# Both feed-forwards with early halves: even features first on one token half, five products more for their pairs, and 24 modulation columns moved into the mixing

## The chip, the cores and the metric

The kernel runs on one core of a Trainium2 chip. The metric is device time in microseconds for one execution. A core has TensorE (matmuls, PE in the profile), VectorE (DVE), ScalarE (ACT), GpSimd (POOL) and SyncE (SP, which here issues the DMAs). Each engine runs its own list of instructions in order and waits on semaphores that others raise. Matmul results go to PSUM, a small memory in banks of 128 x 512 fp32 numbers, which ScalarE and VectorE can read and write too.

## The reference

One layer over 1024 latent tokens and 256 context tokens, width 1024: a half-step feed-forward, a token mixing of two recurrent kinds, a second half-step feed-forward. Every step is modulated by columns computed from the condition vector `c`.

```python
def swiglu(h, w1, w3, w2):
    return (jax.nn.silu(h @ w1) * (h @ w3)) @ w2
...
    m_l = jnp.split(cond_lat @ ada_w[i] + ada_b[i], N_MOD, axis=-1)
    x = x + 0.5 * m_l[2][:, None, :] * swiglu(modulate(rms_norm(x, norm1_w[i]), m_l[0], m_l[1]),
                                                ffn1_w1[i], ffn1_w3[i], ffn1_w2[i])
    ctx = ctx + 0.5 * m_c[2][:, None, :] * swiglu(modulate(rms_norm(ctx, norm1_w[i]), m_c[0], m_c[1]), ...)
    y_l, y_c = token_mixing(modulate(rms_norm(x, norm2_w[i]), m_l[3], m_l[4]), ...)
    x = x + m_l[5][:, None, :] * y_l
    x = x + 0.5 * m_l[8][:, None, :] * swiglu(modulate(rms_norm(x, norm3_w[i]), m_l[6], m_l[7]),
                                                ffn2_w1[i], ffn2_w3[i], ffn2_w2[i])
return rms_norm(x, final_norm_w)
```

The hidden width is 2816, that is 22 features of 128 columns, 11 pairs of features. The modulation `cond_lat @ ada_w` has 72 columns of 128 for the latents, numbered 8m+k for part m and k = 0..7.

## The kernel before, in words

**Numbers.** Every fp32 product is made of three fast matmuls. An operand is split into a high part, written by ScalarE (`whi`, L421), and a low part, the difference, written by VectorE (`wlo`, L422). `mm3` (L426 to L428) then issues high x high, low x high and high x low into one bank. A weight half, `raw`, is a 128 x 512 tile loaded from HBM, split into `whi` and `wlo`; there are six slots of each.

**Seven products.** The activations of 1024 tokens are cut into two token halves and two halves of the inner width. A pair of features makes a 2 x 2 block of weights, and `chain` (L706 ff.) computes the 2 x 2 block product with seven block products in place of eight. A block product, here simply a product, is 4 `mm3`, so 12 matmuls of 128 x 512. The weight combinations are made by VectorE in `seven_w` (L687 to L694), the activation combinations `t1` to `t4` once per feed-forward. Partial results are copied from PSUM by ScalarE (`keep`, L711) and added by VectorE (`plus`, L715). A pair has one chain for w1, whose results go through silu (`c_silu`, L738), and one for w3, whose results are multiplied with it (`c_mul`, L743). When the four gated blocks of a pair are there, `g_out` forms their combinations by subtractions (L751) and stores them to `gd` in HBM (L752), for the products with w2 later. `w2_sums` loads three w2 blocks (L792), adds them and stores the sums.

**The first features.** Before the activations of the second token half are ready, features are computed the classic way, one at a time, half by half: four in the first feed-forward (`first1`, then a loop that finishes token half 1) and two in the second (`first2`). The other 9 and 10 pairs go through `hidden`, which runs w1 chain, modulation work, `w2_sums`, w3 chain, and modulation work again for each pair.

**Modulation.** The 72 latent columns are dot products of a 128 x 1024 block of `adaT` with the condition row: one DMA and one VectorE multiply-and-reduce (L523) each, hung into the chains, `MPER` of them after each chain.

**Order.** In `first1` the three computing engines follow the program's order. In the chains a scheduler orders each engine's list by priority; loads of weights have a raised one (`WPRI`). In the mixing a planner (`Recorder`) records operations and emits a list by its own costs; `SEQ` is the list of steps that it runs through.

Of the kernel before, what the change touches and what calls it, by code (L numbers as in the profile page):

```python
# [392 lines left out]
class Trunk:  # L393
    def __init__(self, ctx, tc, I, out, outt):
        self.tc, self.nc, self.I, self.out, self.outt = tc, tc.nc, I, out, outt
        self.ctx = ctx
        self.uid = 0
        self.ns, self.ndg = NS, 2
        self.cp = ctx.enter_context(tc.tile_pool(name="cp", bufs=1))
        self.hp = ctx.enter_context(tc.tile_pool(name="hp", bufs=1))  # L400
        self.mixd = self.nc.dram_tensor("mixd", (D, LAT), F32, kind="Internal").ap()
        self.xd = self.nc.dram_tensor("xd", (D, LAT), F32, kind="Internal").ap()
        self.gds = [self.nc.dram_tensor(f"gd{i}", (8, NP, P, 512), F32, kind="Internal").ap() for i in range(2)]
        self.sds = [self.nc.dram_tensor(f"sd{i}", (2, NP, P, 512), F32, kind="Internal").ap() for i in range(2)]
        for n, s in (("cgk", (256, CTX)), ("crk", (512, CTX)), ("cgv", (CTX, 512)), ("crv", (CTX, 512)), ("p89d", (P, CTX)), ("s0g", (4, P, P)),
                     ("s0r", (4, P, 2, P)), ("rvd", (P, 8, 256))):
            setattr(self, n, self.nc.dram_tensor(n, s, F32, kind="Internal").ap())
# [135 lines left out]

    def mod_fin(self, j, s, one=False):
# [88 lines left out]
    def norm_t(self, tg, a, b, pool, tp):  # L633
# [8 lines left out]
        for k in range(4):  # L642
            t = self.norm_k(tg, k, a, b, rb, pool)
# [91 lines left out]

    def c_silu(self, f, tg, t, new=False):
# [12 lines left out]
    def g_out(self, f):  # L749
# [11 lines left out]
        put(1, b11), put(2, b21), put(3, b22)  # L761
# [54 lines left out]
    def hidden(self, f0, mods=lambda: None, hold=False):  # L816
        for f in range(f0, NF, 2):
            if hold and f == NF - 2:
                self.held = []
            self.chain(self.w1, f, self.c_silu, self.psA)  # L820
            if f > f0:
                mods()
            self.w2_sums(f // 2 - 1)
            self.chain(self.w3, f, self.c_mul, self.psB)
            if f > f0:
                mods()
# [139 lines left out]
    def ffn_open(self, i, gates, pool):  # L966
        self.w1, self.w3, self.w2 = (self.I[f"w{i}{j}"] for j in (1, 3, 2))
        self.gates_m, self.fp, self.s, self.g = gates, pool, {}, {}
# [176 lines left out]
    def first2(self, tp, diag):  # L1145
        t3 = [self.tile(tp, [P, 512], F32R, f"t3l{k}") for k in range(4)]
        t3 = [tuple(t3[2 * i:2 * i + 2]) for i in range(2)]
        ws = {}
        for f in range(2):
            for i, w in ((0, self.w1), (1, self.w3)):  # L1150
                ws[f, i] = self.load_halves(w[f], t3 if (f, i) == (1, 1) else (None, None))
        raw = []
        for tg in LATTG:
            for f in range(2):
                ps = self.psA()
                mms = self.proj(ws[f, 0], tg, ps)
                if tg == f == 0:
                    self.tc.add_manual_dep(diag.ins, mms[HELD].ins.name, SCHED, reason="order")
                self.c_silu(f, tg, ps, True)
                if tg:  # L1160
                    raw.append(self.t34_raw(2 * f))
                self.c_mul(f, tg, self.H(ws[f, 1], tg))
                if tg:
                    raw.append(self.t34_raw(2 * f + 1))
        return raw

    def first1(self, pools, n1):
# [10 lines left out]
        def fetch(i, q):  # L1178
            raws[i, q] = self.raw_half((self.w1, self.w3)[i % 2][i // 2][:, 512 * q:512 * q + 512])
# [20 lines left out]
        def mms(i, k, js):  # L1200
            w, h = self.wslice(ws[i], k), self.h[0][k]
            for j in js:
                u, v = ((0, 0), (0, 1), (1, 0))[j]
                nc.tensor.matmul(pss[i], w[u], h[v], start=k == 0 and j == 0, stop=k == KD - 1 and j == 1)
# [89 lines left out]
        for st in range(1, KD):  # L1294
# [10 lines left out]
            for i in range(6):  # L1305
                mms(i, st, (0, 2, 1))
                if i == 2 * (st == 1) and n < KD:
# [11 lines left out]
                if n == KD:  # L1319
# [3 lines left out]
                    if i == 2:  # L1323
                        self.c_mul(0, 0, pss[1])
                        self.c_silu(1, 0, pss[2], True)
# [7 lines left out]
        self.c_mul(1, 0, pss[3])  # L1333
        self.c_silu(2, 0, pss[4], True)
        ps = self.psA()
        for k in range(KD):
            if k == 2:
                pr = self.rstd_rows(r, 512, n1, dg=dg)
            self.mm3(ps, self.wslice(ws[6], k), self.h[0][k], k == 0, k == KD - 1)
        rb[1] = self.scr(n1, "nrb")  # L1340
        nc.scalar.copy(rb[1], pr)
        norm_a = lambda k: self.norm_a(1, k, a, b, rb[1], n1, self.x[1][k])
        norm_a(0)
        for k in range(KD):
            if k + 1 < KD:
                norm_a(k + 1)
            if k == 2:
                self.c_mul(2, 0, pss[5])
                self.c_silu(3, 0, ps, True)
            self.norm_b(1, k, b, self.x[1][k])  # L1350
        self.c_mul(3, 0, self.H(ws[7], 0))
        return ws
# [553 lines left out]
    def lat_phase(self, pool):  # L1906
# [32 lines left out]
        cr = lambda: [self.ctx_ret(h, pool) for h in range(4)]  # L1939
        for s in SEQ:  # L1940
            eval(s, {**globals(), **locals()})
        self.late_sg = {h: self.gate_proj(I["wrg"][h], pool) for h in (2, 3)}
# [88 lines left out]
    def run(self):  # L2031
# [26 lines left out]
        self.alloc_h((0, 1), self.hp)  # L2058
        with tc.manual_schedule(engines={mybir.EngineType.PE, mybir.EngineType.DVE, mybir.EngineType.Activation}):
            ws = self.first1((xp, xp, None), n1)  # L2060
            cls("n1"), cls("f1w")
            self.tp = tp = opn("tp")
            t_steps = self.t_make(xp, tp)
            for f in range(4):
                self.c_silu(f, 1, self.H(ws[2 * f], 1), True)
                next(t_steps)
                self.c_mul(f, 1, self.H(ws[2 * f + 1], 1))
                if f % 2:
                    next(t_steps)
# [12 lines left out]
        self.hidden(4, lambda: mods(MPER), True)  # L2082
# [119 lines left out]
        self.x[0] = [rec.wrap(t, xp) for t in self.x[0]]  # L2202
        self.h[2] = [tuple(rec.wrap(t, hc) for t in p) for p in self.h[2]]
# [34 lines left out]
        rec.run()  # L2238
        self.ndg = 2
# [16 lines left out]
        self.T = [[], [], [], []]  # L2256
        for i, raw in enumerate((self.t1r, self.tr)):
            for k in range(4):
                self.t_split(tp, i, k, raw[k])
        raw = self.first2(tp, rec.diags[-4])  # L2260
        late = (None for _ in self.mods_half(f2, (8,)))
# [4 lines left out]
        self.hidden(2, lambda: next(late, None))  # L2266
# [16 lines left out]
HELD = 6  # L2283
EMODS = ((5, (0,)), (2, (0, 1)), (1, (1,)), (0, (1,)), (4, (0, 1)), (3, (0, 1)), (7, (0,)), (6, (0,)))
MPER = 6
# [113 lines left out]
```

## Time and profile before

| what | value |
|---|---|
| time, median of 3 runs | 2084.39 us (2083.61 to 2087.27) |
| the profiled execution | 2088.82 us, span 2087.0 us |
| mean granted TensorE clock | 0.998 |
| TensorE busy | 2071.6 us |
| VectorE busy | 1471.9 us |
| ScalarE busy | 973.3 us |
| HBM read / written | 292.68 MB / 67.24 MB |

A row of the table of costly groups names line, engine, operation, the tile written and the tiles read, the count, the busy time, the mean duration of one, and the idle time of that engine just before, with what ended it. The mean of a pipelined matmul is longer than the distance between two starts, so a matmul's price is taken from the distance. A timeline row gives start, duration, engine, line, operation and count. PEclk is the clock granted to TensorE, as a share of the full one. DMAs appear twice: on the engine that issues them (SPq), and with the time until their data has landed.

### The profile page before, as it was taken

The numbers are of one execution on the slowest core, as the hardware profiler recorded it, in microseconds if no ns is written. First come the engines' busy times: TensorE is split into PE (matmuls) and PEld (weight loads), VectorE is DVE, ScalarE is ACT, GpSimd is POOL, SyncE is SP. The second block draws the span as 40 slices with busy tenths as digits, with TensorE's granted clock in tenths as the row PEclk, the third lists the DMA queues.
The fourth block names the chain that finished last, engine by engine and source line by source line (L and its number), as shares of the span: only waits on it lengthen the run. The fifth ranks groups of instructions, "written<-read, shape, count | busy, mean of one in ns | idle before, by whom it ended". The sixth has DMA issues, their size and how long they took to land.

```text
span 2087.0 us, 34162 instructions
## 1 busy us (share of the span) xinstructions
PE 2071.6 (99%) x12352; PEld 1763.0 (84%) x12352; DVE 1471.9 (71%) x2660; ACT 973.3 (47%) x1818; POOL 199.3 (10%) x195
## 2 busy tenths in 40 slices
PE   9999999999999999999999999999999999999998
PEld 6888888888889999998788988888888888888888
DVE  6889999666776445765577478767776666765586
ACT  5433433435544445566475246444434344344553
POOL 0000000000015665001021001000000000010000
PEclk9999999999999999999999999999999999999999
DMA  9277667449886553674233233242344444477774
GB/s 348 84 241 237 232 217 256 149 165 371 277 289 222 181 183 115 195 219 129 76 108 98 79 91 105 90 162 81 112 156 147 144 163 157 151 235 229 218 237 151
DMA packets 201082, 370.58 MB, mean 178 GB/s; under 512 B 23249, under 2 KB 35921, under 8 KB 200785
## 3 DMA queue, kind: packets, MB, share of 16 engines
q1 hardware_dynamic: 200768, 368.33, 53.7%
q8 instruction: 97, 1.59, 0.3%
q14 instruction: 73, 0.59, 0.1%
q10 hardware_dynamic: 144, 0.07, 0.0%
HBM read 292.68 MB, written 67.24 MB: 172 GB/s over the span
## 4 chain that ended last, share of the span: by engine, by line
PE 77%; DVE 10%; DMA 8%; issue 3%; ACT 1%; SPq 0%; DVEq 0%; POOLq 0%; ACTq 0%
PE psa L147 18%; PE psa L426 10%; PE psa L428 10%; PE psa L427 10%; PE psb L147 9%; PE psb L427 7%; PE psb L428 7%; PE psb L426 7%; DVE junk L523 2%; DVE wlo L422 2%; DMA raw<-in_w 2%; DMA raw<-sd 2%; DVE hl L422 1%; DMA raw<-gd 1%; DMA hl<-sd 1%
## 5 line engine op out<-in xcount | busy, mean ns | idle before, releaser
L421 ACT ACTIVATE whi<-raw 128x512 fp32r<-128x512 f32 x371 | 233.9, 631 | 502.7 <-issue 160.6
L422 DVE TENSOR_TENSOR wlo<-raw,whi 128x512 fp32r<-128x512 f32 x371 | 254.1, 687 | 178.0 <-ACT whi L421 175.6
L426 PE MATMUL psa<-hh,whi 128*128 128x512 f32 x684 | 267.0, 390 | 1.2 <-ACT s L738 0.6
L428 PE MATMUL psa<-hh,wlo 128*128 128x512 f32 x684 | 266.3, 389 | 0.0
L427 PE MATMUL psa<-hl,whi 128*128 128x512 f32 x684 | 266.2, 389 | 0.0
L427 PE MATMUL psb<-hl,whi 128*128 128x512 f32 x568 | 221.6, 390 | 0.5 <-DVE hl L422 0.3
L428 PE MATMUL psb<-hh,wlo 128*128 128x512 f32 x568 | 221.3, 390 | 0.2 <-DVE wlo L422 0.2
L426 PE MATMUL psb<-hh,whi 128*128 128x512 f32 x568 | 221.1, 389 | 0.0
L426 PEld LDWEIGHTS psa<-hh,whi 128*128 128x128 f32 x684 | 128.4, 188 | 28.9 <-ACT s L711 1.7
L147 DVE TENSOR_TENSOR wlo<-raw,whi 128x512 fp32r<-128x512 f32 (+1 forms) x140 | 88.5, 647 | 90.8 <-ACT whi L147 80.1
L147 PE MATMUL psa<-hl,whi 128*128 128x512 f32 x384 | 152.5, 397 | 0.0
L147 PE MATMUL psa<-hh,whi 128*128 128x512 f32 x384 | 152.3, 397 | 0.0
L147 PE MATMUL psa<-hh,wlo 128*128 128x512 f32 x384 | 152.2, 396 | 0.0
L428 PEld LDWEIGHTS psa<-hh,wlo 128*128 128x128 f32 x684 | 128.4, 188 | 26.6
L427 PEld LDWEIGHTS psa<-hl,whi 128*128 128x128 f32 x684 | 128.5, 188 | 26.3
L422 POOL TENSOR_TENSOR hl<-s,hh 128x512 fp32r<-128x512 f32 x88 | 132.4, 1530 | 145.2 <-DVE hl L422 81.1
L147 ACT ACTIVATE whi<-raw 128x512 fp32r<-128x512 f32 (+1 forms) x140 | 82.5, 599 | 119.7 <-PE psa L147 94.1
L427 PEld LDWEIGHTS psb<-hl,whi 128*128 128x128 f32 x568 | 106.6, 188 | 24.7 <-DVE hl L422 2.7
L428 PEld LDWEIGHTS psb<-hh,wlo 128*128 128x128 f32 x568 | 106.6, 188 | 23.1 <-DVE wlo L422 1.2
L426 PEld LDWEIGHTS psb<-hh,whi 128*128 128x128 f32 x568 | 106.6, 188 | 22.2
L428 PE MATMUL psa<-hh,hl 128*128 128x256 f32 x392 | 111.1, 284 | 0.0
L426 PE MATMUL psa<-hh,hh 128*128 128x256 f32 x392 | 111.1, 283 | 0.0
(443 smaller groups left out, 4820.4 us busy)
## 6 DMA issues: line engine op xcount, KB each, us to landing
raw<-in_w SPq DMA_DIRECT2D x242, 256.0 KB, 3.3
s<-in_w SPq DMA_DIRECT2D x198, 256.0 KB, 3.7
gd<-s SPq DMA_DIRECT2D x154, 256.0 KB, 2.8
ada<-in_adaT SPq DMA_DIRECT2D x60, 512.0 KB, 4.6
raw<-gd SPq DMA_DIRECT2D x91, 256.0 KB, 3.5
sd<-s SPq DMA_DIRECT2D x44, 256.0 KB, 2.7
raw<-sd SPq DMA_DIRECT2D x44, 256.0 KB, 3.2
hh<-in_w SPq DMA_DIRECT2D x44, 256.0 KB, 4.0
```

Of the source, the lines that this page charges most:

```text
L147: self.rec.add(self.eng, lambda: f(*map(get, a), **{x: get(v) for x, v in k.items()}), outs, ins, name, a, k)
L421: nc.scalar.activation(hi, src, AF.Copy)
L422: (eng or nc.vector).tensor_tensor(out=lo, in0=src, in1=hi.bitcast(F32), op=ALU.subtract)
L426: mm(ps, wa[0], xa[0], start=start, stop=False, skip_group_check=more)
L427: mm(ps, wa[0], xa[1], start=False, stop=False, skip_group_check=more)
L428: return mm(ps, wa[1], xa[0], start=False, stop=stop, skip_group_check=more)
L523: nc.vector.tensor_tensor_reduce(out=self.junk, in0=t, in1=self.cs[s], scale=1.0, scalar=self.col("ada_b")[:, j:j + 1], op0=ALU.mult, op1= ...
```

## The change

**Early halves.** For the even feature of eight pairs in the first feed-forward (0, 2, ... 14) and of five in the second (0, 2, ... 8), the four products on token half 0 are computed first: w1 and w3, each on the lower and then on the upper half of the inner width. The first half-sum, called c1, is one of the seven products; ScalarE copies it from PSUM when the lower half is done, and it is stored to `c1d` in HBM (`c1_keep`). The bank then goes on to the full sum, which is the feature's result for token half 0; the gated block is stored to `gd` (`g_part`).

**The rest.** `rest` computes the remaining five products of such a pair, for w1 and for w3. c1 is loaded again (line 826 of the changed kernel) and copied by ScalarE into the PSUM bank (line 844), on which the first product, with w6, accumulates. With w3, the stored gated block is loaded again as well (line 829).

**The features done the classic way** are no longer there, and all 11 pairs go through `hidden`, the early ones with `rest`, the others with `chain`. The matmuls of 128 x 512 number 7079 before and 7007 after.

**Modulation.** 24 columns (parts 5, 7, 6) leave the first feed-forward and become 48 half columns in the mixing (`mods_mix`): a 256 KB DMA and a 128 x 512 multiply-and-reduce each, three after each entry of `SEQ`. `MPER` becomes 2 for early pairs and 5 for the others. The normalised second token half is no longer split in its lower four blocks, which only feed combinations.

The diff, cut to its core:

```diff
+    def mods_mix(self, pool):
+        for o in (0, 512):
+            row = self.tile(self.cp2, [P, 512], F32, "wgr")
+            nc.sync.dma_start(row, self.I["c"][:, o:o + 512].broadcast_to([P, 512]))
+            nc.scalar.activation(row, row, AF.Silu)
+            for j in [8 * m + k for m in MMODS for k in range(KD)]:
...
+                t = self.t2(pool)
+                nc.sync.dma_start(t, self.I["adaT"][j][:, o:o + 512])
+                nc.vector.tensor_tensor_reduce(out=t, in0=t, in1=row, scale=1.0, scalar=m if o else self.col("ada_b")[:, j:j + 1],
+                                               op0=ALU.mult, op1=ALU.add, accum_out=m)
...
+    def prod4(self, wh, b, ps, start, stop=True):
+        for k in range(4):
+            self.mm3(ps, [t[:, k * P:(k + 1) * P] for t in wh], b[k], start and k == 0, k == 3, not start)
+
+    def part(self, f):
+        ws = [self.load_halves(w[f]) for w in (self.w1, self.w3)]
+        ps = self.psA(), self.psB()
+        mms = []
+        for i in range(2):
+            for k in range(4):
+                mms.append(self.mm3(ps[i], self.wslice(ws[i], k), self.h[0][k], k == 0, k == 3))
+            self.c1_keep(f, i, ps[i])
+        for i in range(2):
+            self.prod4(ws[i][1], self.h[0][4:], ps[i], False)
+            (self.c_mul if i else self.c_silu)(f, 0, ps[i], True)
+        self.g_part(f)
+        return mms
...
+    def c1_keep(self, f, i, ps):
+        t = self.stile()
+        self.nc.scalar.copy(t, ps)
+        self.nc.sync.dma_start(self.c1d[i, f // 2], t)
...
+    def rest(self, w, f, out, bank):
+        nc, i = self.nc, int(w is self.w3)
+        with self.tc.high_priority(offset=WPRI):
+            c1 = self.stile()
+            nc.sync.dma_start(c1, self.c1d[i, f // 2])
+            if i:
+                self.g[f, 0] = self.stile()
+                nc.sync.dma_start(self.g[f, 0], self.gd[1, f // 2])
+                self.again.add(f)
+            w6, w5, w7, w3, w4 = self.five_w(w, f)
+        t1, t2, t3, t4 = self.T
...
+        a, b = bank(), bank()
+        nc.scalar.copy(a, c1)
+        self.prod4(w6, t2, a, False)
+        u2 = keep(a)
+        self.prod4(w5, t1, b, True)
+        c5 = keep(b)
+        self.prod4(w7, t3, a, False)
+        u3 = keep(a)
+        out(f + 1, 1, plus(c5, u3, c5))
+        self.prod4(w3, self.h[1][4:], b, False)
+        out(f, 1, plus(u2, b, u2))
+        self.prod4(w4, t4, a, False)
+        out(f + 1, 0, a, True)
...
-    def hidden(self, f0, mods=lambda: None, hold=False):
+    def hidden(self, f0, mods=lambda: None, hold=False, parts=0):
...
-            self.chain(self.w1, f, self.c_silu, self.psA)
+            chain = self.rest if f < parts else self.chain
+            chain(self.w1, f, self.c_silu, self.psA)
...
+        cols = self.mods_mix(pool)
         for s in SEQ:
             eval(s, {**globals(), **locals()})
+            for _ in range(MMPER):
+                next(cols, None)
...
-        self.hidden(4, lambda: mods(MPER), True)
+        self.hidden(0, mods, True, 8 + 2 * len(PARTS))
...
-HELD = 6
+HELD = 3
...
-MPER = 6
+MMPER = 3
+MMODS = (5, 7, 6)
+MPER = (2, 5)
+PARTS = (8, 10, 12, 14)
```

In the lists that follow, a row has the line, the operation, the tile written and the tiles read; `gd`, `sd` and `c1d` are stores in HBM, `in_w` the weights. First SyncE's list in the first feed-forward, where one pair ends and the next begins. Before:

```order
L752 DMA gd<-s_1927 128x512
L752 DMA gd<-s_2097 128x512
L663 DMA raw_2464<-in_w 128x512
L752 DMA gd<-s_2100 128x512
L752 DMA gd<-s_1868 128x512
L752 DMA gd<-s_2105 128x512
```

After:

```order
L681 DMA raw_2743<-in_w 128x512
L873 DMA gd<-s_2337 128x512
L873 DMA gd<-s_2466 128x512
L873 DMA gd<-s_2469 128x512
L826 DMA s_2483<-c1d 128x512
L873 DMA gd<-s_2279 128x512
L873 DMA gd<-s_2474 128x512
```

The load of c1 for the next w1 chain, `s_2483`, stands behind three stores of the gated blocks; s_2337 is written by the multiply of the pair's last product, s_2466 and s_2469 by the first two subtractions after it.

ScalarE's list and then TensorE's at the same place. Before, where the pair's last bank is psb_2671 and the next w1 chain writes psa_2842 and psa_2843:

```order
L421 ACTIVATE whi_2838<-raw_2805 128x512
L421 ACTIVATE whi_2976<-raw_2967 128x512
L421 ACTIVATE whi_2981<-raw_2973 128x512
L711 COPY s_2856<-psa_2842 128x512
L711 COPY s_2870<-psa_2843 128x512
```

```order
L427 MATMUL psb_2671<-hl_222_1122,whi_2667 128x512
L428 MATMUL psb_2671<-hh_221_1121,wlo_2668 128x512
L426 MATMUL psa_2842<-hh_16_114,whi_2810 128x512
L427 MATMUL psa_2842<-hl_17_115,whi_2810 128x512
L428 MATMUL psa_2842<-hh_16_114,wlo_2811 128x512
```

After, where psa_2518 is the bank of w6 and psa_2519 that of w5:

```order
L422 ACTIVATE whi_2625<-raw_2613 128x512
L844 COPY psa_2518<-s_2483 128x512
L422 ACTIVATE whi_2629<-raw_2619 128x512
L836 COPY s_2533<-psa_2518 128x512
L422 ACTIVATE whi_2633<-raw_2615 128x512
```

```order
L428 MATMUL psb_2390<-hl_264_1164,whi_2386 128x512
L429 MATMUL psb_2390<-hh_263_1163,wlo_2387 128x512
L427 MATMUL psa_2519<-t1h_196_883,whi_2501 128x512
L427 MATMUL psa_2518<-t2h_192_879,whi_2497 128x512
L428 MATMUL psa_2518<-t2l_193_880,whi_2497 128x512
```

The copy of c1 into the bank (L844) is new on ScalarE, and TensorE has one matmul of the w5 product, and then those of w6, which write the bank after the copy.

SyncE's list inside a pair, between the w1 and the w3 chain. Before:

```order
L663 DMA raw_2808<-in_w 128x512
L792 DMA s_2620<-in_w 128x512
L792 DMA s_2621<-in_w 128x512
L792 DMA s_2622<-in_w 128x512
L513 DMA ada_643_3284<-in_adaT 128x1024
L663 DMA raw_2967<-in_w 128x512
```

After:

```order
L681 DMA raw_2870<-in_w 128x512
L915 DMA s_2599<-in_w 128x512
L915 DMA s_2600<-in_w 128x512
L915 DMA s_2601<-in_w 128x512
L826 DMA s_2609<-c1d 128x512
L829 DMA s_2611<-gd 128x512
L681 DMA raw_2872<-in_w 128x512
```

Here the load of c1 for the w3 chain and that of the gated block come behind a raw load, whose slot is set free by a weight split, and three w2 loads.

More of the change, by code (lines that the diff above doesn't have):

```diff
@@ L760, in g_out @@
         b11, b12, b21, b22 = (g.pop((f + i, t)) for i in range(2) for t in LATTG)
-        put(1, b11), put(2, b21), put(3, b22)
+        if f not in self.again:
+            put(1, b11)
+        put(2, b21), put(3, b22)
         t1 = self.stile()
@@ L1143, in t_make @@
         yield
[L1145 to L1165, printed above, removed]
     def first1(self, pools, n1):
@@ L1203, in mms @@
                 u, v = ((0, 0), (0, 1), (1, 0))[j]
-                nc.tensor.matmul(pss[i], w[u], h[v], start=k == 0 and j == 0, stop=k == KD - 1 and j == 1)
+                nc.tensor.matmul(pss[i], w[u], h[v], start=k == 0 and j == 0, stop=k % 4 == 3 and j == 1, skip_group_check=k > 3)
         def sums(j, o):
@@ L2238, in run @@
         rec.run()
+        self.mod = mod
         self.ndg = 2
@@ L2256, in run @@
         self.T = [[], [], [], []]
+        mms = self.part(0)
+        tc.add_manual_dep(rec.diags[-4].ins, mms[HELD].ins.name, SCHED, reason="order")
+        self.part(2)
         for i, raw in enumerate((self.t1r, self.tr)):
@@ L2259, in run @@
                 self.t_split(tp, i, k, raw[k])
-        raw = self.first2(tp, rec.diags[-4])
-        late = (None for _ in self.mods_half(f2, (8,)))
+        self.part(4)
+        self.part(6)
+        raw = [self.t34_raw(k) for k in range(4)]
+        self.part(8)
         for k in range(4):
@@ L2265, in run @@
             self.t4_split(k, raw[k][1])
-        self.hidden(2, lambda: next(late, None))
+        late = (None for _ in self.mods_half(f2, (8,)))
+        self.hidden(0, lambda n: next(late, None), False, 10)
         for _ in late:
```

156 lines of the change are left out of this document (118 added, 38 removed).

## The prediction

> **What bounds the kernel now.** I read the page's busy times first, then its clock row.
>
> ```profile
> span 2087.0 us, 34162 instructions
> PE 2071.6 (99%) x12352; PEld 1763.0 (84%) x12352; DVE 1471.9 (71%) x2660; ACT 973.3 (47%) x1818; POOL 199.3 (10%) x195
> PEclk9999999999999999999999999999999999999999
> ```
>
> TensorE is busy for 99% of the span at the full clock, so work taken off it shows one for one, and so does any stretch in which it stands still. The table of busy time by stretch, for TensorE alone, asks how much slack the feed-forwards have: the seven-product chains of the first, the opening of the second, and the chains of the second.
>
> ```profile
> 114.37:460.33 345.96, 345.13 (x1514) 1.00 0.65 215
> 1432.81:1479.41 46.60, 46.01 (x209) 1.00 0.12 40
> 1479.41:1860.21 380.80, 380.80 (x1681) 1.00 0.47 156
> ```
>
> The last row is the ideal: 380.80 us / 1681 matmuls = 0.2265 us each, without one wait. In the first row 1514 x 0.2265 = 342.9, so 3.0 us are stalls. Next the timeline at one seam, where a pair's w3 chain ends and the next pair's w1 chain begins (TensorE, VectorE, ScalarE, then the DMA queue):
>
> ```profile
> 1555.35 0.39 PE L428 MATMUL psb<-hh,wlo 128*128 128x512 f32 x1
> 1555.57 0.39 PE L426 MATMUL psa<-hh,whi 128*128 128x512 f32 x1
> ...
> 1553.84 0.68 DVE L422 TENSOR_TENSOR wlo<-raw,whi 128x512 fp32r<-128x512 f32 x1
> 1555.77 0.69 DVE L743 TENSOR_TENSOR s<-psb,s 128x512 f32<-128x512 f32 x1
> 1556.38 0.68 DVE L422 TENSOR_TENSOR wlo<-raw,whi 128x512 fp32r<-128x512 f32 x1
> 1556.98 0.68 DVE L751 TENSOR_TENSOR s<-s,s 128x512 f32<-128x512 f32 x1
> ...
> 1558.85 0.57 ACT L711 COPY s<-psa 128x512 f32<-128x512 f32 x1
> ...
> 1554.54 0.33 SPq L663 DMA_DIRECT2D raw<-in_w  x1
> 1555.87 3.34 SPq L752 DMA_DIRECT2D gd<-s  x4
> 1559.27 0.42 SPq L537 DMA_DIRECT2D s<-in_adaT  x1
> ```
>
> Call S the start of the pair's last matmul (1555.35). TensorE passes the seam without a pause, because nothing the next chain needs comes through what follows S. SyncE does not pass it: its stores of the gated products wait one by one for VectorE's multiply and subtractions. They begin at S+0.52 and hold it until S+3.92, so anything behind them is issued four microseconds late. How long a load then takes, from the page's list of DMA issues:
>
> ```profile
> raw<-in_w SPq DMA_DIRECT2D x242, 256.0 KB, 3.3
> s<-in_w SPq DMA_DIRECT2D x198, 256.0 KB, 3.7
> raw<-gd SPq DMA_DIRECT2D x91, 256.0 KB, 3.5
> ada<-in_adaT SPq DMA_DIRECT2D x60, 512.0 KB, 4.6
> ```
>
> **The change part by part.**
>
> *Matmuls taken away.* A product is 12 matmuls. Before, the first feed-forward runs four features the classic way (32 products) and nine pairs at 14; the second two features (16) and ten pairs at 14. After, every pair costs 14, since an early half takes four and its rest ten. That is four and two products less, 72 matmuls: 72 x 0.2265 = -16.3 us, all on the path.
>
> *The seam between pairs (w3 to w1), 11 times* (seven in the first feed-forward, four in the second). The first product of a rest (w6) now adds to a bank that ScalarE fills from c1, and c1 comes by a DMA that stands on SyncE behind three stores of the pair just ended. Queued behind that wait: ScalarE's copy, and TensorE, which has only one matmul of w5 pulled ahead of it. After S, VectorE runs a split, two multiplies and two subtractions before the third store may go. The rows put the first at S+0.42 and the next ones 0.60 apart, so the fifth starts at S+2.8 and ends at S+3.5; the store takes 0.4, and the load of c1 is issued at S+3.9, as the old row behind its stores was at S+3.92. It lands 3.5 later (S+7.4) and the copy takes 0.57 (S+8.0). TensorE ran out of work at S+0.45 (two matmuls of 0.2265). Idle 7.6 us; 11 x 7.6 = 84 us. Bounds: 6.1 (VectorE 1.2 earlier, two operations fewer ahead of the subtractions; landing 3.2 to 3.3) and 8.7 (landing 4.6, as for the larger load). I take 7.6, because the size and the queue are those of the 3.5 us row. With both ends 67 to 96.
>
> *The seam inside a pair (w1 to w3), 13 times.* In nine of them the load of c1 stands behind a raw load that waits for a split, and three w2 loads. The old row has such a raw load at S-0.81, right when the split of 1553.84 ends (1554.52). Four issues of 0.33 to 0.42 put c1 at S+0.7; plus 3.5, plus 0.57, less the 0.45 that TensorE still had: idle 4.4 us, 9 x 4.4 = 40. Two more have less ahead of them and I put them at 3.1, and in the last two c1 is there and only the split and copy on ScalarE stand in the way, 0.63 + 0.57 = 1.2. Together 40 + 6 + 2 = 48 us; bounds 32 (a load that is issued 1.2 earlier) and 62 (landing 4.6).
>
> *The early halves.* In the first feed-forward they share VectorE with the sums of activations and the modulation columns:
>
> ```profile
> 150.00:200.00 50.00, 49.76 (x218) 40.41 (x217) 49.88 (x85) 17.95 (x32) 0.00 (x0) 1.00 0.70 228
> 1000.00:1050.00 50.00, 48.04 (x615) 39.35 (x615) 30.04 (x70) 23.79 (x55) 1.02 (x1) 0.97 0.23 68
> L523 DVE CUSTOM_DVE_ANT_0 junk<-ada,condc,cols 128x1024 bf16<-128x1024 f32 x54 | 68.9, 1277 | 6.0 <-DMA ada<-in_adaT 4.1 <-ACT condc L455 1.7
> ```
>
> Columns here: TensorE, weight loads, VectorE, ScalarE, GpSimd. VectorE has 0.12 us of 50 to spare in the old chains at that point. The 24 columns that leave the stage relieve it by 24 x 1.277 = 31 us, so the old 3.0 us of stalls in the chains go (-3). But inside the early halves eight of the remaining 1.28 us reductions stand among the weight splits that TensorE waits for: between 2 (nearly all covered) and 10 (each in the way once); I take +6. In the opening of the second feed-forward the copies of the half-sums stand on ScalarE behind work that waits for the norm. Its old row has 0.59 us of idle in all; five early halves at that rate give 3, and a wait of three or four such operations for two of them 9; I take +6.
>
> *Mixing.* The 24 columns come back as 48 half reductions. At half the 1.277 us and a fixed tenth, 48 x 0.7 = 34 us of VectorE, in stretches where it has 20 of 50 us free: hidden, unless one stands ahead of a wanted operation. The order has 22 more changes between kinds of matmul; the timeline shows what one costs.
>
> ```profile
> 1033.71 0.48 PE L147 MATMUL psa<-hh,whi 128*128 128x512 f32 x1
> 1034.03 0.39 PE L147 MATMUL psa<-hl,whi 128*128 128x512 f32 x1
> 1034.26 0.39 PE L147 MATMUL psb<-p89T,wg 128*128 128x512 f32 x1
> ```
>
> The first after a change takes 0.32 to the next start, the second 0.23: 22 x 0.09 = 2. I take +3; bounds 0 and 12 (a third of the reductions in the way).
>
> *The clock.* The old kernel has one pause of TensorE above 1 us, and this is what followed (its timeline row, then two-microsecond stretches: TensorE busy, granted clock, DMA share, GB/s):
>
> ```profile
> 1024.60 0.33 PE L147 MATMUL psb<-zq,zk 128*32 128x32 f32 x16 [1.63 <-issue]
> ...
> 1022.00:1024.00 2.00, 0.76 (x53) 1.00 0.41 128
> 1024.00:1026.00 2.00, 1.40 (x36) 0.84 0.04 11
> 1026.00:1028.00 2.00, 2.00 (x14) 0.50 0.00 0
> 1028.00:1030.00 2.00, 2.00 (x51) 0.81 0.00 0
> 1030.00:1032.00 2.00, 2.00 (x70) 1.00 0.03 8
> ```
>
> After 1.63 us of idle the grant fell to half and was back some 3.5 us later. Lost: 2 x (0.16 + 0.50 + 0.19) = 1.7 us. The new seams leave 20 pauses of 4.4 us or more. If each is followed by the same, 20 x 1.7 = +34 us; bounds 0 (after dense work the clock holds) and 37 (the two of 3.1 us as well). I take 34, since the only pause in the trace longer than a microsecond did it and these are nearly three to five times as long.
>
> [...]
>
> *Sum.* -16.3 + 84 + 48 - 3 + 6 + 6 + 3 = +128, and +34 = +162 us on the profiled execution. This took 2088.8 us against a median of 2084.4, so from the median: 2084.4 + 162 = 2246 us.
>
> **The rivals.**
>
> *The clock holds.* Pauses within dense work may be watched otherwise than that one among small matmuls. Then 2084.4 + 128 = 2212 us.
>
> *c1 is there in time.* If SyncE runs far enough ahead that the loads pass before the stores block, only ScalarE's split and copy stand at a seam: 26 x 1.2 = 31 us and no clock drop; 2084.4 - 16.3 + 31 - 3 + 15 = 2111 us. Against it: the old row of four stores shows SyncE held for 3.34 us after S, and the order has the load behind three of them.
>
> *The copy hides too, and the saving shows.* TensorE's queue would have to find other work for the copy's time. Price: the matmuls alone, -16.3 - 3 and at least the lower bounds of the openings (+5): 2070 us, faster. This decides where the mean idle of the 26 seams is under 16.3 / 26 = 0.63 us, about one copy. For it speaks only that TensorE today passes every seam without a pause; against it, that the copy must precede all but one to three of the matmuls that follow.
>
> *VectorE becomes the bound of the openings and of mixing,* with their upper bounds (10 + 9 + 12 in place of 15): 16 us more, 2262 us. Against it stand the 20 free microseconds in 50.
>
> **How the numbers follow.** The forecast 0.52 (its own range 2205 to 2285, from the bounds of the two seams), the clock holds 0.24, c1 in time 0.10, all hidden 0.06, VectorE besides 0.05, and 0.03 for something near no change. A difference below 0.2%, 4 us, can't be told from none. So faster 0.06, same 0.02, slower 0.92. The range starts at 2150: with the clock held and both seams at their lower bounds the time is 2212 - 17 - 16 = 2179, and 2150 lies some way from there towards c1 in time, for seams of which a part is met in time. It ends at 2290: the forecast with 12, 14 and 16 more from the upper bounds is 2288. It leaves out the three cases from 2111 down to no change and below, 0.19 together, and next to nothing above.
>
> **What the new profile would show.** TensorE's busy share near 92%. In the table of costly groups the first matmul of a product (hh,whi, or t2h's group) with some 130 us of idle before it, released by ScalarE's copy of line 844, and that copy in turn waiting for the DMA from c1d. On the chain that ended last a DMA row s<-c1d. At a seam the load of c1 issued about 4 us after S, and 7 to 8 us without a matmul. PEclk digits of 8 or less through both chains if the clock falls, 9 throughout if not. In mixing no new wait of TensorE on VectorE above a few us in all. Wrong would be: loads of c1 that land before S; a w6 product that starts with no wait; or a span that grows in mixing instead.

## The result and the profile after

The changed kernel takes 2317.71 us (median of 6 runs, 2313.42 to 2323.59) against 2084.86 us beside it. The ratio is 1.1116, with a 95% interval of 1.1098 to 1.1135. The forecast was 2246 us with a range of 2150 to 2290: the direction and the place were right, and the size fell short by 72 us, 28 us outside the range.

The page of the changed kernel, first its busy times and its slices:

```profile
span 2318.5 us, 34479 instructions
PE 2119.8 (91%) x12280; PEld 1784.9 (77%) x12280; DVE 1494.9 (64%) x2734; ACT 1008.4 (43%) x1882; POOL 206.2 (9%) x195
PE   9877676799999999999999999998766699999998
PEclk9987878899999999999999999999978899999999
```

TensorE executes 72 matmuls fewer and is busy for longer, 2119.8 us against 2071.6, because part of its time ran at a lower clock: the mean granted one is 0.954 against 0.998. The dips of TensorE, and within them those of its clock, lie in two places: the slices from about 60 to 460 us and from about 1570 to 1850 us, the early halves and the rests of the two feed-forwards. The table of waits, for TensorE and for ScalarE (what waited for what: us in total, times, longest), says what stood there:

```profile
PE psa L427 <- ACT psa L844: 99.4, 13, 10.9
PE psb L427 <- ACT psb L844: 64.5, 11, 7.5
PE psa L427 <- ACT s L778: 14.6, 5, 4.9
...
ACT psa L844 <- DMA s<-c1d: 90.3, 12, 9.4
ACT psb L844 <- DMA s<-c1d: 52.7, 13, 6.1
```

L844 is the copy of c1 into the PSUM bank; its 26 copies are the only writes to a bank in this trace besides those of the matmuls (VectorE reads a bank in 457 instructions and writes none). TensorE waits 164 us for it, and the copy itself spends 143 us waiting for c1 to land. L778 is the copy of a half-sum in the openings.

A seam between two pairs in the first feed-forward and one in the second (timelines of TensorE, ScalarE and SyncE; S, the start of the pair's last matmul, is 307.55 in the first and 1721.24 in the second):

```profile
307.55 0.39 PE L429 MATMUL psb<-hh,wlo 128*128 128x512 f32 x1
307.78 0.39 PE L427 MATMUL psa<-t1h,whi 128*128 128x512 f32 x1
316.12 0.80 PE L427 MATMUL psa<-t2h,whi 128*128 128x512 f32 x1 [7.95 <-ACT psa L844]
...
315.47 0.59 ACT L844 COPY psa<-s 128x512 f32<-128x512 f32 x1 [7.04 <-DMA s<-c1d]
...
310.39 1.65 SPq L873 DMA_DIRECT2D gd<-s  x3
312.08 0.44 SPq L826 DMA_DIRECT2D s<-c1d  x1
```

```profile
1732.19 0.79 PE L427 MATMUL psa<-t2h,whi 128*128 128x512 f32 x1 [10.33 <-ACT psa L844]
...
1731.55 0.59 ACT L844 COPY psa<-s 128x512 f32<-128x512 f32 x1 [9.43 <-DMA s<-c1d]
...
1724.08 2.85 SPq L873 DMA_DIRECT2D gd<-s  x5
1726.98 0.44 SPq L538 DMA_DIRECT2D s<-in_adaT  x1
1727.47 0.58 SPq L826 DMA_DIRECT2D s<-c1d  x1
```

In the first, three stores hold the load of c1 until S+4.5, and it lands 3.4 us later. In the second, five stores and another load stand ahead: S+6.2, 4.1 us to land, and a pause of 10.3 us. And a seam inside a pair (S = 331.89):

```profile
338.87 0.80 PE L427 MATMUL psb<-t2h,whi 128*128 128x512 f32 x1 [6.37 <-ACT psb L844]
...
338.23 0.59 ACT L844 COPY psb<-s 128x512 f32<-128x512 f32 x1 [4.98 <-DMA s<-c1d]
...
331.21 0.33 SPq L681 DMA_DIRECT2D raw<-in_w  x1
331.59 1.37 SPq L915 DMA_DIRECT2D s<-in_w  x3
333.01 0.43 SPq L826 DMA_DIRECT2D s<-c1d  x1
```

Here the load is issued at S+1.1, but it is the fifth of a burst within 2.2 us, and the copy can start only 5.2 us later.

The table of busy time by stretch, TensorE alone (length, busy, matmuls, granted clock, then DMA share and GB/s): the rests of the first feed-forward, the mixing, the rests of the second, then the two-microsecond steps after the pause shown above, and last the mixing of the kernel before.

```profile
124.00:469.90 345.90, 244.93 (x924) 0.83 0.46 156
1004.50:1569.40 564.90, 563.77 (x4663) 1.00 0.47 144
1635.00:1848.00 213.00, 149.45 (x564) 0.81 0.36 120
1730.00:1732.00 2.00, 0.00 (x0) 0.50 0.22 84
1732.00:1734.00 2.00, 1.81 (x4) 0.50 0.00 0
1734.00:1736.00 2.00, 2.00 (x6) 0.50 0.00 0
1736.00:1738.00 2.00, 2.00 (x6) 0.50 0.00 0
1738.00:1740.00 2.00, 2.00 (x10) 1.00 0.11 16
```

```profile
865.72:1432.80 567.08, 564.33 (x4663) 1.00 0.40 121
```

The clock is at half after the pause and stays there for almost six more microseconds of work. The mixing, with 48 half columns more, is 2.2 us shorter.

Summed over the starts of the matmuls in the two traces (a distance over 0.6 us counts as a pause, what a shorter one has above 0.2265 us as slow), the two feed-forwards come out so:

| after minus before, us | first feed-forward | second |
|---|---|---|
| 48 and 24 matmuls less | -10.9 | -5.4 |
| pauses | +116.0 | +75.6 |
| slow matmuls | +35.2 | +25.0 |
| sum | +140.3 | +95.2 |
| measured to the next stage's start | +139.9 | +95.2 |

With the mixing's -2.2 and -1.1 in the stages between them the whole is 231.8 us, and the spans differ by 231.5.

### The profile page after: what moved, and what is told of

It reads as the page before. It is cut to its first block, busy times and chain, and to the rows that moved or that the text cites. A ratio compares the mean times of both kernels' runs of the same rounds, so it can differ in the third digit from the quotient of the medians.

```text
span 2318.5 us, 34479 instructions
## 1 busy us (share of the span) xinstructions
PE 2119.8 (91%) x12280; PEld 1784.9 (77%) x12280; DVE 1494.9 (64%) x2734; ACT 1008.4 (43%) x1882; POOL 206.2 (9%) x195
## 4 chain that ended last, share of the span: by engine, by line
PE 79%; DVE 7%; DMA 6%; issue 4%; ACT 2%; SPq 1%; POOL 0%; DVEq 0%; POOLq 0%; ACTq 0%
PE psa L147 15%; PE psa L427 10%; PE psa L428 10%; PE psa L429 10%; PE psb L427 9%; PE psb L428 9%; PE psb L429 9%; PE psb L147 6%; DMA s<-c1d 4%; DVE wlo L423 1%; ACT whi L422 1%; DVE s L872 1%; DVE s L864 1%; DMA raw<-in_w 1%; DVE junk L524 1%
## 5 line engine op out<-in xcount | busy, mean ns | idle before, releaser
L423 DVE TENSOR_TENSOR wlo<-raw,whi 128x512 fp32r<-128x512 f32 x391 | 268.4, 689 | 399.1 <-ACT whi L422 398.5
L422 ACT ACTIVATE whi<-raw 128x512 fp32r<-128x512 f32 x391 | 245.9, 631 | 584.0 <-PE psb L428 180.2
L427 PE MATMUL psa<-hh,whi 128*128 128x512 f32 x628 | 248.2, 395 | 15.6 <-ACT s L778 14.6
L429 PE MATMUL psa<-hh,wlo 128*128 128x512 f32 x628 | 247.2, 394 | 0.0
L428 PE MATMUL psa<-hl,whi 128*128 128x512 f32 x628 | 247.2, 394 | 0.0
L427 PE MATMUL psb<-hh,whi 128*128 128x512 f32 x584 | 228.1, 391 | 2.3 <-ACT whi L422 2.3
L427 PEld LDWEIGHTS psa<-hh,whi 128*128 128x128 f32 x628 | 119.2, 190 | 43.5 <-ACT s L778 16.7
L147 PE MATMUL psa<-hh,whi 128*128 128x512 f32 x384 | 152.2, 397 | 0.0
L147 PE MATMUL psa<-hl,whi 128*128 128x512 f32 x384 | 152.1, 396 | 0.0
L147 PE MATMUL psa<-hh,wlo 128*128 128x512 f32 x384 | 152.1, 396 | 0.0
L429 PEld LDWEIGHTS psa<-hh,wlo 128*128 128x128 f32 x628 | 119.4, 190 | 25.8 <-DVE wlo L423 0.9
L428 PEld LDWEIGHTS psa<-hl,whi 128*128 128x128 f32 x628 | 119.3, 190 | 24.4
L427 PE MATMUL psa<-t2h,whi 128*128 128x512 f32 x66 | 34.1, 517 | 99.4 <-ACT psa L844 99.4
```

Of the source, the lines that this page charges most:

```text
L147: self.rec.add(self.eng, lambda: f(*map(get, a), **{x: get(v) for x, v in k.items()}), outs, ins, name, a, k)
L422: nc.scalar.activation(hi, src, AF.Copy)
L423: (eng or nc.vector).tensor_tensor(out=lo, in0=src, in1=hi.bitcast(F32), op=ALU.subtract)
L427: mm(ps, wa[0], xa[0], start=start, stop=False, skip_group_check=more)
L428: mm(ps, wa[0], xa[1], start=False, stop=False, skip_group_check=more)
L429: return mm(ps, wa[1], xa[0], start=False, stop=stop, skip_group_check=more)
```

## The experiments

All times stand beside runs of the kernel before on the same chip; ratios are to these. The diffs are against the changed kernel, or against the experiment that is named.

**The products in another order.** The w5 product goes first, and its split with it:

```diff
-        r = [self.half(a11), self.half(s1), self.half(a21)]
+        w5 = self.half(s1)
+        r = [self.half(a11), w5, self.half(a21)]
...
         a, b = bank(), bank()
-        nc.scalar.copy(a, c1)
-        self.prod4(w6, t2, a, False)
-        u2 = keep(a)
         self.prod4(w5, t1, b, True)
         c5 = keep(b)
+        nc.scalar.copy(a, c1)
+        self.prod4(w6, t2, a, False)
+        u2 = keep(a)
```

> In the rest of a pair the w5 product goes ahead of the w6 product; nothing else is changed. Theory: the pause at a seam ends when c1 has landed and been copied, so 11 more matmuls ahead of the wait (2.5 us) shorten each of 23 pauses by 2.5 us: 2317.7 - 58 = 2260 us, with the clock still falling at nearly all of them. Rival (the copy's place on ScalarE is the cost and not the load): 2.7 us of cover hide a split and a copy of 1.2 us altogether, and the pauses vanish: about 2100 us.

Measured: 2203.04 us, ratio 1.0559 (1.0543 to 1.0575). That is 57 us better than the theory gave and 100 worse than the rival. Its waits of TensorE:

```profile
PE psa L427 <- ACT psa L847: 29.0, 11, 5.6
PE psa L427 <- ACT s L837: 17.3, 18, 1.0
PE psa L427 <- ACT s L778: 10.5, 5, 4.9
PE psb L427 <- ACT s L837: 9.2, 9, 1.0
...
PE psb L427 <- ACT psb L847: 2.8, 4, 1.3
```

The wait for c1 (L847 here) falls from 164 to 32 us, more than twice as much as 2.5 us a seam, and new small ones for ScalarE's other copies (L837) appear. The order of TensorE's list shows the greater part of why. Free of any wait, the w5 product of a chain is drawn forward into the chain before, and part or all of w3 goes ahead of w6. After a chain's last product come ten matmuls of a later w5 and then, at seven of the eleven seams between pairs, the twelve of w3, before w6 starts: 22 matmuls or 5.0 us of cover in place of one, not the 12 I had counted. Inside pairs it is 18, at the other four seams 15, and at these four pauses of 5.4 to 6.0 us are left. On the mean 17.5 matmuls more, 24 x 4.0 = 95 us, make up most of the fall of 132 us; the rest is not accounted for, though the new small waits stand partly ahead of w6 and pass while c1 is on its way. w3 in its turn waits for the copy of the w5 bank, which stands behind splits on ScalarE. With shorter pauses the mean granted clock was 0.987, against 0.954 in the changed kernel. That the pause follows the load is supported; place and product are told apart by the next runs.

**c1 loaded one chain early.** The order of the products stays; only the load is emitted before the chain ahead of the one that uses it:

```diff
+    def c1_load(self, f, i):
+        with self.tc.high_priority(offset=WPRI):
+            self.c1s[f, i] = self.stile()
+            self.nc.sync.dma_start(self.c1s[f, i], self.c1d[i, f // 2])
...
-            c1 = self.stile()
-            nc.sync.dma_start(c1, self.c1d[i, f // 2])
+            c1 = self.c1s.pop((f, i))
...
+            if f < parts:
+                self.c1_load(f, 1)
             chain(self.w1, f, self.c_silu, self.psA)
...
+            if f + 2 < parts:
+                self.c1_load(f + 2, 0)
             chain(self.w3, f, self.c_mul, self.psB)
```

> c1 is loaded one chain earlier (before the chain ahead of the one that uses it); the order of the products stays. Theory (the load is issued late because it stands behind stores and loads that wait): the pauses of 6 to 11 us shrink to what ScalarE's split and copy take, 1.2 to 1.8 us, 23 x 1.3 = 30 us in all, and the clock no longer falls: 2317.7 - 168 (pauses) - 53 (slow matmuls) + 30 = 2127 us. Rival (the load is late because the DMA queues are full, wherever it stands): pauses of over 4 us stay and the time is above 2230 us.

Measured: 2129.90 us, ratio 1.0213 (1.0196 to 1.0230), where the theory said 2127 and the rival above 2230. One edit of where a DMA stands takes 188 us. What is left of the wait for the copy of c1 is L848 in its waits, and the clock is back at 0.993:

```profile
PE psa L427 <- ACT s L840: 19.1, 15, 2.6
PE psa L427 <- ACT s L778: 18.0, 5, 5.7
PE psa L427 <- ACT psa L848: 2.0, 2, 1.6
PE psb L427 <- ACT s L840: 1.6, 3, 1.0
```

So it is the place of the load in SyncE's list that makes c1 late, and not how full the DMA queues are. The copy of c1, which is still there, makes TensorE wait 2 us in all once c1 is in time. The 20 us for L840 are waits for the copies of other partial results. That they come later on ScalarE because it has one copy more per chain is likely and was not tested by itself.

**Both edits.**

> Both edits. Theory: w5 hides ScalarE's copy as well, so no seam costs anything: 2317.7 - 168 - 53 = 2097 us, TensorE at the full clock through both chains, and what is left above 2084.4 - 16.3 = 2068 lies in the openings. Rival (full queues): no better than the w5 product ahead alone, about 2250 us.

Measured: 2124.22 us, ratio 1.0185 (1.0170 to 1.0200); the theory said 2097. The w6 products wait for nothing, but w3 waits for the copy of the w5 bank (18.2 us in 13 waits), so the second edit is worth 6 us and not 30. Half of this expectation failed: another copy on ScalarE took the place of the one that was hidden.

**The first feed-forward alone.** The opening and the chains of the second as before the change (two features by the old `first2`, ten pairs by seven products):

```diff
...
-        self.part(4)
-        self.part(6)
-        raw = [self.t34_raw(k) for k in range(4)]
-        self.part(8)
+        raw = self.first2(tp, rec.diags[-4])
...
-        self.hidden(0, lambda n: next(late, None), False, 10)
+        self.hidden(2, lambda n: next(late, None))
```

> The second feed-forward as before the change (two classic features, ten pairs by seven products, its lower blocks of token half 1 split again in the norm); the first feed-forward and the mixing as changed. Theory: the two feed-forwards lose time each for itself, and the second one's 95 us go: 2317.7 - 95 = 2223 us. Rival (the second one's loss hangs on what the first or the mixing leave late): more than 10 us away from that.

Measured: 2222.08 us, ratio 1.0656 (1.0640 to 1.0672). 95.6 us come back, the 95.2 of the table: each feed-forward loses for itself.

**c1 kept out of PSUM.** On top of the early load, w6 starts its bank afresh, and VectorE adds c1 to the results:

```diff
-        nc.scalar.copy(a, c1)
-        self.prod4(w6, t2, a, False)
-        u2 = keep(a)
+        self.prod4(w6, t2, a, True)
+        u2 = plus(self.stile(), a, c1)
...
-        u3 = keep(a)
-        out(f + 1, 1, plus(c5, u3, c5))
+        plus(c5, c5, c1)
+        out(f + 1, 1, plus(c5, a, c5))
...
-        out(f + 1, 0, a, True)
+        out(f + 1, 0, plus(c1, a, c1))
```

> c1 loaded one chain early, and no longer copied into PSUM: w6 starts its bank afresh, and VectorE adds c1 to the three results that need it (three more adds of 0.6 us and three ScalarE copies less per chain). Theory (what is left at the seams is the wait for ScalarE's copies, some 25 us in all): 2130 - 25 = 2105 us, and no product waits for ScalarE at a seam. Rival (VectorE, full between 100 and 250 us, becomes the bound): 26 x 1.8 = 47 us more of VectorE, of which a third or more shows in the first feed-forward: 2115 us or above, with waits for wlo.

Measured: 2092.32 us, ratio 1.0035 (1.0022 to 1.0048), 13 us better than the theory's 2105. The table by stretch, all engines, in the pairs where VectorE was said to become the bound (TensorE, weight loads, VectorE):

```profile
150.00:200.00 50.00, 50.00 (x222) 41.21 (x221) 49.58 (x86) 15.34 (x26) 0.00 (x0) 1.00 0.81 276
200.00:250.00 50.00, 50.00 (x221) 40.93 (x220) 49.52 (x81) 15.51 (x26) 0.00 (x0) 1.00 0.70 239
```

TensorE has no pause at a seam any more. VectorE is as full as it can be and still in time. The pauses in the chains fell by the 25 us that I had counted. I had not counted the slow matmuls behind the longest pauses, 8 us, nor a pause of 5.9 us in the second opening, which shrank to 1.0.

**Less modulation in the early pairs.** On the kernel before this: `MPER = (0, 8)` in place of `(2, 5)`.

> As the no-preload kernel, and the modulation columns of the first feed-forward leave its early pairs (0 after each of their chains instead of 2, and 8 instead of 5 after the others). If VectorE binds in the early pairs, this gives back 5 to 15 us against the kernel beside it; if not, the two are the same within 3 us.

Measured: 2092.68 us, ratio 1.0037 (1.0023 to 1.0052): the same. VectorE binds nothing there, as its full but punctual rows said.

**The splits of activation sums later**, in the opening of the second feed-forward, by one and by two features (on the no-preload kernel):

```diff
-        for i, raw in enumerate((self.t1r, self.tr)):
-            for k in range(4):
-                self.t_split(tp, i, k, raw[k])
         self.part(4)
+        for i, raw in enumerate((self.t1r, self.tr)):
+            for k in range(4):
+                self.t_split(tp, i, k, raw[k])
         self.part(6)
```

> As the no-preload kernel, and in the second feed-forward the eight splits of activation sums come after the fourth feature's early half instead of before it. Theory (the opening's pauses are ScalarE's copies of half-sums standing behind splits that wait for the norm): the pauses of 5.3 and 4 to 6 us there shrink, 6 to 10 us less with the clock than the no-preload kernel. Rival (the early halves need activations that the norm has not made yet, whatever the order): no difference above 2 us.

> As the one before, with the eight splits one feature further back. If the splits in the way are the cause, the same or 1 to 4 us better; if they are now too late for the first pair's rest, a new pause of a few us ahead of it and 2 to 6 us worse.

Measured: 2093.18 us (ratio 1.0036, 1.0023 to 1.0049) and 2091.97 us (1.0034, 1.0022 to 1.0045): no difference, and the longest wait for L778 is 4.9 us in both as before. Moving the lines did not move the copies: in ScalarE's list they still stand behind the last splits and the last activation of the norm, presumably since the scheduler puts there what it takes to be ready first. These two runs tried nothing of the cause; a wait had to be taken from TensorE instead.

**A bank of its own for the first upper half.** In `part`, for the first feature of the second feed-forward only, on the no-preload kernel:

```diff
...
+            t = self.c1_keep(f, i, ps[i])
+            if sep:
+                ps[i] = t
...
+            if sep:
+                ps2 = (self.psB if i else self.psA)()
+                self.prod4(ws[i][1], self.h[0][4:], ps2, True)
+                o = self.stile()
+                self.nc.vector.tensor_tensor(out=o, in0=ps[i], in1=ps2, op=ALU.add)
+            else:
+                self.prod4(ws[i][1], self.h[0][4:], ps[i], False)
...
```

> As the no-preload kernel (c1 early, c1 added by VectorE); in the opening of the second feed-forward the upper half of the first feature goes to banks of its own and VectorE adds the kept half-sum, so that TensorE need not wait for ScalarE's copy. Theory (that one wait of 4.9 us and the slow clock after it, 2.9 us, are what the copy costs there): 5 to 8 us less, 2085 us. Rival (the next feature's copies only take its place): less than 2 us.

Measured: 2085.90 us, ratio 1.0002 (0.9993 to 1.0011): 6.4 us less, as the theory said.

**The sums and splits of activations dealt out evenly** in the first feed-forward's early halves, and the silu of the context row after them:

```diff
...
-                    if i:
-                        next(steps, None)
+                    next(steps, None)
...
             self.split(x1[k], *one[k])
+            if k == 1:
+                yield
...
-            self.nc.scalar.activation(t, t, AF.Silu)
+            x = self.nc.scalar.activation(t, t, AF.Silu)
+            if after is not None:
+                self.tc.add_manual_dep(x.ins, after.ins.name, SCHED, reason="order")
```

> As the no-preload kernel; in the first feed-forward the sums and splits of activations are dealt out after every product of the early halves instead of every second, in eleven portions instead of six, and ScalarE's silu of the context row, which waits for a DMA, comes after the early halves. Theory (the pauses there are copies and weight splits behind portions that wait for VectorE): 4 to 9 us less, 2086 us. Rival (VectorE is full there, whatever the order): less than 2 us.

Measured: 2086.34 us, ratio 1.0006 (0.9997 to 1.0015): 6.0 us less. The pauses there have become one of 3.5 us. Which of the two edits did it was not tried.

**Both of these.**

> Both of these edits. If they are independent and the theory holds for both: 2092 - 7 - 6 = 2079 us, below the kernel before by 5 us. If neither holds: 2092 us.

Measured: 2079.13 us, ratio 0.9973 (0.9964 to 0.9982), faster than the kernel before by 0.27%. The page:

```profile
span 2079.2 us, 34446 instructions
PE 2059.3 (99%) x12280; PEld 1749.4 (84%) x12280; DVE 1534.2 (74%) x2814; ACT 968.2 (47%) x1804; POOL 200.2 (10%) x195
PE   9999999999999999999999999999999999999998
```

With the same 12280 matmul records as the changed kernel, TensorE's busy time is 12.3 us below that of the kernel before, and most of this arrives in the span. This version keeps everything the change set out to do, with the early load, the adds of c1, and the two openings mended.

**Without the early load, c1 out of PSUM.** Does the early load still matter once c1 is no longer copied into PSUM?

> c1 is added by VectorE and not copied into PSUM, but its load stays at the late place behind the stores. TensorE then meets c1 only through the bank: the third product (w7) may not write it before VectorE has read the first one's sum, 24 matmuls or 5.4 us after the seam. With the landing times of the changed kernel (7.5 us after S between pairs in the first feed-forward, 10 in the second, 6.3 inside pairs) and 0.6 for the add, pauses of some 2.5, 5 and 1.5 us are left: 7 x 2.5 + 4 x 5 + 11 x 1.5 = 54 us, and the clock falls at the longest: 2092 + 54 + 10 = 2156 us. Rival (with c1 out of TensorE's way its load may come when it will): 2092 us.

Measured: 2115.20 us, ratio 1.0141 (1.0124 to 1.0158). Neither number: 23 us above the kernel with the early load, 41 below what I expected. Its waits of TensorE:

```profile
PE psa L427 <- ACT s L778: 10.5, 4, 4.9
PE psa L427 <- DVE s L840: 8.7, 9, 1.9
PE psa L427 <- ACT s L836: 5.8, 6, 1.0
```

L840 is the add that waits for c1. The load's late place still shows, but inside a pair the order of TensorE's list has the next chain's w6 and w5 products ahead of the old chain's last three. So some 48 matmuls stand between a chain's first product and w7, twice what I had counted, to get over the landing. Freed of the copy, the scheduler finds cover of its own; with the early load nothing is left to cover. Against the changed kernel each edit alone brings most of the time back: the early load 188 us, the adds in place of the copy 203 us, both 225 us. So the loss needs both, a load that comes late and a first product that cannot start without it; removing either is nearly enough.

## Why the prediction was right or wrong

The chain of waits was as forecast: load, copy, first product, and the clock after it. What failed is the size of four terms of the sum, all too low: the clock by 26 us, the seam inside a pair by 21 (with 3 us that no term had), the seam between pairs by 15 and the openings by 12. The mixing came out 6 us below its term, with the stages beside it. Together that is 68 of the 70 us by which the two traces differ beyond the +162 us of the sum.

**The seam between pairs: mechanism right, price too low.** The load of c1 behind the stores, ScalarE's copy behind the load and TensorE with one matmul in hand were all there. The 11 pauses add up to 99 us in the trace, where I put 84. In the first feed-forward the one quoted comes to 8.0 us against 7.6, as SyncE reached the load at S+4.5 and not S+3.9: VectorE had a weight combination (L819) more ahead of the subtractions. Two of the seven there are 9.0 and 11.0 us, with the load at S+5.7 and S+5.4. The step that failed is that I took one list for all eleven: in the second feed-forward the load stands behind five stores and a modulation load, and three of its four pauses are 10.2 to 10.5 us.

**The seam inside a pair: mechanism right, a term of it mis-sized.** 66 us in eleven pauses where I put 48 in thirteen; the last two did not show, and the first rest of each feed-forward, which the sum left out, adds 3. The nine full ones are 6.8 us in the mean against 4.4. I had c1 issued at S+0.7 (it was S+0.7 to S+1.6) and landing in 3.5 us, the median over the whole kernel. As the last of five or six loads issued within 2.2 to 2.7 us it took 4.8 to 5.8 us. Between pairs of the first feed-forward, behind stores, it took 3.1 to 3.4 us in six of seven cases. So a median is the price of a typical load; that the burst is what made this one longer fits these numbers and was not tested by itself.

**The clock: right that it falls, price too low.** 60 us of slow matmuls against 34. The 21 pauses above 5 us each cost 1.5 to 3.0 us of slow matmuls after them, 2.3 in the mean, 48 us together, where the one old case had given 1.7; the slow stretch lasted 3 to 6 us here and 3.5 us there. Five shorter pauses, of 2.5 to 3.7 us between two starts, cost 10 us more, though two of 2.2 and 2.6 us cost nothing. Why one slow stretch is twice as long as another stays open. The rival in which the clock holds through dense work is refuted. So is the reading that a pause like the old one always suffices. That one was 1.63 us of idle, 1.83 us from start to start. Within the feed-forwards of the changed kernel distances of up to 1.6 us between two starts left the clock alone, those of 2.2 to 3.7 us went either way (2.55 us without a loss, 2.54 us with one of 1.8), and all 21 from 5.3 us on brought it down. The trace shows a band and not a sharp edge. Of a slow stretch about half is lost: 12 matmuls at 0.43 us are a stretch of 5.2 us and lose 2.4.

**The openings: too low.** 24 us of pauses (13 and 11) where I put 12 in all, with bounds of 5 and 19. Of them 14.6 us, in five waits, are waits for the copies of half-sums, most of which stand on ScalarE behind splits that wait for VectorE; the two experiments on the openings got 12 us back, the slow matmuls included.

**The mixing: wrong in sign, small.** -2.2 us against +3, below its bounds of 0 and 12; why it became shorter was not tried. The 48 half reductions took 0.75 us each in the mean, where I put 0.7.

**The matmuls taken away: right.** -10.9 and -5.4 us in the table above, -16.3 together; in the mended version TensorE's busy time falls by 12.3 us.

**The rivals.** c1 in time (2111 us) did not happen by itself, and the early load shows what it would have been: 2130 us. That all is hidden and the saving shows (2070 us, decided below 0.63 us a seam) is what the mended version nearly is, at 2079. VectorE as the bound of the openings and of mixing (2262 us) was half right: the pauses of the openings passed their upper bounds, through copies behind splits that wait for VectorE, and the mixing did not. All four sizes erred on the same side, since I priced each new wait by the old kernel's undisturbed rows; the range, built from bounds around these, ended 28 us short. The forecast's own range, 2205 to 2285, was not quite what its bounds give, which for the two seams is 2213 to 2272.

## What to carry to other kernels

A load that a chain needs at its first instruction belongs in the issuing engine's list ahead of the stores of the work before it: read its place in that list at every kind of seam, and count what waits ahead of it, since one place costs 8 us and another 10. Price a load in a burst by the burst (here 4.8 to 5.8 us to its landing, against 3.1 to 3.4 behind the stores), and add some two microseconds for the clock to a pause of TensorE above 5 us (1.5 to 3.0 in the changed kernel's trace). Before an accumulation is preloaded into PSUM, ask whether an add on another engine would leave the matmuls free to start: here that took the copy, the wait and a scheduler's constraint away together, and brought back 203 us even with the load left late.

## What was not expected of the hardware

The half-speed stretch after a pause varied from 6 to 14 matmuls of 0.43 us (1.5 to 3.0 us lost) for pauses of nearly the same length, in one run and the same loop: 14 after one of 6.5 us from start to start, 6 after one of 6.6. VectorE at 49.5 of 50 us for 100 us in a row delayed no matmul of the no-preload kernel: TensorE was busy for all 100.
